# Channel-major products of a hybrid encoder layer as three 256-column matmuls into one sum, with the large operands at one byte offset

## The chip, the core and the metric

The kernel runs on one core of a Trainium2 chip. The engines of the core are TensorE (PE in the profile; PEld is its loading of weights), VectorE (DVE), ScalarE (ACT), GpSimd (POOL) and SyncE (SP). The metric is the device time of one launch in microseconds.

## What is computed

One layer of an encoder on 256 tokens of 2048 channels, all in float32. Cut to what matters here:

```python
n = rms_norm(h, norm_mix_w)
proj = einsum("bsd,dp->bsp", n, w_in)            # 2048 -> 13344 channels
#   q, k, v of 8 delta heads (conv, silu), z, gates; 3 branches of q, k, v for 8 dilated heads
mixed = concatenate([delta_mixer(...), dilated_mixer(...)], -1)
h = h + einsum("bsm,md->bsd", mixed, w_out)      # 2048 -> 2048
n = rms_norm(h, norm_ffn_w)
up = depthwise_conv_centered(einsum("bsd,df->bsf", n, w_ffn_in), conv_ffn_w)   # 2048 -> 11264
gate, val = split(up, 2, -1)
h = h + einsum("bsf,fd->bsd", silu(gate) * val, w_ffn_out)                     # 5632 -> 2048
return rms_norm(h, norm_final_w)
```

## The kernel before

Every float32 operand of the large products is split in two float32r numbers: a high part and the rest. A product is then three products: high x high, low x high and high x low. The activations n are kept transposed in `xcat`, a tile of 128 partitions x 16 slices k x 512 columns: of each slice the first 256 columns are the high part of the 256 tokens, the last 256 the low part.

Weights come from HBM in pieces of 1 MB into four buffers `raw`, issued from the SP queue (line 254). A piece serves two items (or two halves of a longer list). For each item ScalarE makes the high part (`hi`, line 263) and VectorE the rest (`lo`, line 264), 128 x 1024 elements each, in four buffers each, three items ahead of the matmuls (`LA = 3`). The order of the work on each engine is the order in which the program writes it. `run_items` walks over the items: it splits ahead, calls the `done` of the item before, issues the matmuls of this item, and then lets background generators (convolutions, the delta rule, attention, norms) issue some work, up to a budget per item on VectorE and ScalarE (`BV`, `BA`).

There are four kinds of large products:

- channel-major blocks (`cm_block`, lines 314 and 317): the weights are the stationary operand and `xcat` the moving one, so the result has channels on partitions. A block of 128 channels takes two items, with 16 steps over k. Each step is one matmul of 512 columns (`hi` against both halves of `xcat`) and one of 256 (`lo` against the first half). The 512 columns of the accumulator bank so hold two sums, which `evac` (lines 331 to 339) adds: ScalarE copies the second half into a small tile `tmp`, VectorE adds the first half and writes the result. 80 blocks of w_in and 88 blocks of w_ffn_in are made in this way, 2688 steps in all.
- token-major blocks of v (`v_slab`, lines 392 to 394): `xcat` is stationary, `hi` and `lo` are moving, 256 columns each, 1152 matmuls.
- w_out and w_ffn_out (`tm_group`, lines 1231 to 1233): `mxh`/`mxl` or `gth`/`gtl` are stationary, `hi` and `lo` moving, 512 columns each.
- a small product for the gates (lines 460 and 461), 32 channels wide, in 16 steps.

Blocks of w_in alternate between two accumulator banks, so the matmuls of a block wait until the block two before it has been read out. From the up-projection on there are four such banks. After the up-projection `up_hook` (lines 1380 to 1387) does as `evac` does, and then multiplies by `rbc` into a padded tile for the convolution.

The delta rule's solve, its scan and the attention run beside these products in the first half. The profile's lines L960 to L1050 are the scan, L1160 to L1211 the attention.

Of the kernel before, what the change touches and what calls it, by code (L numbers as in the profile page):

```python
# [4 lines left out]
F32 = mybir.dt.float32  # L5
F32R = mybir.dt.float32r
I32 = mybir.dt.int32
AF = mybir.ActivationFunctionType
ALU = mybir.AluOpType

P = 128
T = 256
D = 2048
KT = D // P
# [69 lines left out]
def block_kernel(tc, A, out, dbg=None):  # L84
# [4 lines left out]
    ACT = nc.scalar.activation  # L89
    V = nc.vector  # L90
    G = nc.gpsimd
    mm = nc.tensor.matmul
# [15 lines left out]
    def pool(name, **kw):  # L108
        g = tc.tile_pool(name=name, bufs=1, reuse_waits="tile", **kw)
        return g, g.__enter__()  # L110
# [5 lines left out]
    gw, wp = pool("weights", side="left")  # L116
    gx, xp = pool("xcat", side="right")
# [25 lines left out]
    raws = [wp.tile([P, 2048], F32, name=f"raw{i}") for i in range(NR)]  # L143
    his = [wp.tile([P, 1024], F32R, name=f"hi{i}") for i in range(NU)]
    los = [wp.tile([P, 1024], F32R, name=f"lo{i}") for i in range(NU)]
    tmps = [wp.tile([P, T], F32, name=f"tmp{i}") for i in range(2)]
    xcat = xp.tile([P, KT, 512], F32R, name="xcat")

    rec_d = dram.tile([H, P, 1536], F32, name="rec_d")
    z_d = dram.tile([H, P, T], F32, name="z_d")  # L150
# [4 lines left out]


    gens = []
    state = {"tmp": 0, "n": 0, "v": 0.0, "a": 0.0}
    done = set()

    def spawn(g, prio=1):
        gens.append((prio, len(gens) + state["n"], g))
        state["n"] += 1000
        gens.sort(key=lambda t: t[:2])
# [40 lines left out]
    def grab(slots):  # L205
        n = 0
        while not slots.free:
            pump(1e9, 1e9)
            n += 1
            assert n < 10000  # L210
        if n:
            state["forced"] = state.get("forced", 0) + 1
        return slots.get()
# [83 lines left out]
    def next_acc():  # L297
        accn[0] += 1
        return accs[accn[0] % len(accs)]

    def cm_block(ch, j, done, width=P):

        box = {}

        def half(kh):
            def mms(hi, lo):
                if kh == 0:
                    box["acc"] = next_acc()
                acc = box["acc"][:width]
                for kk in range(8):  # L310
                    k = kh * 8 + kk

                    def a():
                        mm(acc[:, :512], lhsT=hi[:, kk, :], rhs=xcat[:, k, :], start=k == 0, stop=k == KT - 1)  # L314

                    def b():
                        mm(acc[:, :T], lhsT=lo[:, kk, :], rhs=xcat[:, k, :T], start=False, stop=False)  # L317

                    if k == KT - 1:
                        b(), a()  # L320
                    else:
                        a(), b()

            return mms

        for kh in range(2):
            Item(ch[kh], lambda t, j=j: t[:, :, j * width : (j + 1) * width], half(kh),
                 (lambda: done(box["acc"])) if kh else None)

    def evac(out_ap, acc, n=P, perm=None):  # L330

        tmp = tmps[state["tmp"] % 2]
        state["tmp"] += 1
        ACT(tmp[:n], acc[:n, T:512], AF.Copy)
        a, b = acc[:n, :T], tmp[:n]
        if perm:
            a = a.rearrange("p (c m) -> p c m", c=4)
            b = b.rearrange("p (c m) -> p c m", c=4)
        V.tensor_add(out_ap, a, b)  # L339

    def natural(ap):

# [21 lines left out]
    g_hi = x0.tile([P, KT, 32], F32R, name="g_hi")  # L364
# [91 lines left out]
    gacc = next_acc()  # L456

    def gate_mms(k2):
        for k in (2 * k2, 2 * k2 + 1):
            mm(gacc[:32, :512], lhsT=g_hi[:, k, :], rhs=xcat[:, k, :], start=k == 0, stop=False)  # L460
            mm(gacc[:32, :T], lhsT=g_lo[:, k, :], rhs=xcat[:, k, :T], start=False, stop=k == KT - 1)

    for k2 in range(8):
        bk = DB.get()
        for e in range(2):
            k = 2 * k2 + e
            for q in range(2):
                nc.tensor.transpose(bk[:, e * T + q * P : e * T + (q + 1) * P], xs[q][:, k * P : (k + 1) * P], ident)
        if k2 >= 3:
            gate_mms(k2 - 3)  # L470
        for e in range(2):
            k = 2 * k2 + e
            src = bk[:, e * T : (e + 1) * T]
            ACT(xcat[:, k, :T], src, AF.Copy, scale=nw_mix[:, k : k + 1])
        for e in range(2):
            k = 2 * k2 + e
            src = bk[:, e * T : (e + 1) * T]
            stt(xcat[:, k, T:], src, nw_mix[:, k : k + 1], xcat[:, k, :T].bitcast(F32), op0=ALU.mult, op1=ALU.subtract)
        DB.put(bk)
        if k2 in (4, 7):  # L480
            split(prog["split"])
            prog["split"] += 1
    run_items(1)
    for k2 in range(5, 8):
        gate_mms(k2)
# [15 lines left out]
    def gate_hook(acc):  # L501
        gg_, gpool = pool("gates", side="right")
        graw = gpool.tile([32, T], F32, name="graw")
        evac(natural(graw), acc, n=32, perm=True)
        spawn(g_gates(graw, gg_, gpool), 0)
# [155 lines left out]
    def qkv_hook(which, h, acc):  # L661
        pad = grab(pads)
        evac(natural(pad[:, 2 : T + 2]), acc, perm=True)
        spawn(g_conv(which, h, pad))
# [125 lines left out]
    def z_hook(h, acc):  # L790
        if h == 6:
            z_pads()
        pad = grab(pads)
        evac(natural(pad[:, 2 : T + 2]), acc, perm=True)

        def g():
            yield 0
            zt = yield from take(zts)
            ACT(zt[:, 64:T], pad[:, 2 : T - 62], AF.Silu)
            ACT(zt[:, 0:64], pad[:, T - 62 : T + 2], AF.Silu)  # L800
            pads.put(pad)
            nc.gpsimd.dma_start(z_d[h], zt)
            done.add(("z", h))
            later(4, lambda: zts.put(zt))
            yield (0, 450)

        spawn(g(), 0)
# [257 lines left out]
    gl, lp = pool("dil", side="right")  # L1065
# [3 lines left out]
    sms = [lp.tile([P, 512], F32, name=f"sm{i}") for i in range(2)]  # L1069
    PT = lp.tile([P, 4, 2, P], F32, name="PT")  # L1070
    smal = lp.tile([P, 2, 4], F32, name="smal")
    swap = [(i + 16) % 32 for i in range(32)]

    def g_tables():
# [185 lines left out]
    rbc = rC  # L1260
# [90 lines left out]
    for c in range(2):  # L1351
        k0 = FT - 8 + 4 * c
        ch = Chunk(w_down[k0 * P : (k0 + 4) * P, 3 * 512 :].rearrange("(k p) c -> p k c", p=P), (4, 512))
        for u in range(2):
            i = 2 * c + u
# [23 lines left out]

    def up_hook(which, f, acc):  # L1380
        pad = grab(fpad)
        tmp = tmps[state["tmp"] % 2]
        state["tmp"] += 1
        ACT(tmp, acc[:, T:512], AF.Copy)
        V.tensor_add(tmp, acc[:, :T], tmp)
        V.tensor_mul(pad[:, 1 : T + 1], tmp, rbc)
        spawn(g_up(which, f, pad))

    hooks["up"] = up_hook
# [2 lines left out]
    def g_up(which, f, pad):  # L1392
        yield 0
        y = yield from take(fy)
        b = which * FT + f
        ACT(y, pad[:, 0:T], AF.Copy, scale=cwf[:, 0, b : b + 1])
        yield 0
        for d in (1, 2):
            stt(y, pad[:, d : d + T], cwf[:, d, b : b + 1], y, op0=ALU.mult, op1=ALU.add)  # L1399
        fpad.put(pad)  # L1400
        yield 700
        if which == 0:
            ACT(y, y, AF.Silu)
            gate_t[f] = y
            yield 0
        else:
            while f not in gate_t:
                yield 0
            g = gate_t.pop(f)
            V.tensor_mul(y, y, g)  # L1410
            fy.put(g)
            yield 300
            ACT(gth[:, f, :], y, AF.Copy)
            V.tensor_sub(gtl[:, f, :], y, gth[:, f, :].bitcast(F32))
            fy.put(y)
            yield 700
# [79 lines left out]
```

## Time and profile before

| | us |
|---|---|
| median of 3 runs | 1555.35 (1553.68 to 1556.74) |
| the profiled execution | 1554.66 |
| its span | 1552.9 |
| PE busy | 1522.1 (98%) |
| PEld busy | 1326.1 (85%) |
| DVE busy | 1102.1 (71%) |
| ACT busy | 848.3 (55%) |
| matmuls of lines 314 and 317 | 2688 each |
| matmuls of lines 392 to 394 | 384 each |
| matmuls of lines 1231 to 1233 with mxh, mxl | 128 each |

Matmuls overlap in the profile: a record is longer than the time after which the next one starts (a 128x512 matmul lasts 398 ns on average). What a matmul takes of the path is read from the distance between two starts, or from how many start in a window, and not from the duration of one.

### The profile page before, as it was taken

The page shows a single profiled execution, that of the slowest core. Times are in us where ns is not written, and L with a number is a line of the kernel's source. Part 1 is how long each engine was busy: PE and PEld are TensorE (multiplying, and loading weights), DVE is VectorE, ACT ScalarE, POOL GpSimd, SP SyncE. Part 2 cuts the span into 40 slices and gives each one's busy share as a digit, 9 for nine tenths or more (in the row PEclk, how much of TensorE's full clock was granted, in tenths as well). Part 3 has the DMA queues.
Part 4 walks back from the last instruction along what each step waited for, and adds up shares of the span by engine and source line. Part 5 has one row for each costly group of instructions (what it writes and reads, how often), then busy time and mean ns, then how long its engine had stood idle before and what let it go on. Part 6 is the DMA issues. An engine that isn't in the chain of part 4 may idle for free.

```text
span 1552.9 us, 23123 instructions
## 1 busy us (share of the span) xinstructions
PE 1522.1 (98%) x8827; PEld 1326.1 (85%) x8827; DVE 1102.1 (71%) x1872; ACT 848.3 (55%) x1518; POOL 163.4 (11%) x245
## 2 busy tenths in 40 slices
PE   7999997999999999999999999999999999999997
PEld 6878886898998898898788888888888888888886
DVE  5878986978965776676557777777777777455454
ACT  5587773555555555654546555555555555344342
POOL 3263442000012202100000000000000000000000
PEclk9999999999999999999999999999999999999999
DMA  9656689655658646554765555656565657566552
GB/s 256 217 171 207 221 264 216 215 172 163 190 145 243 217 129 197 183 163 160 245 205 177 191 189 184 196 170 210 165 206 173 202 179 246 198 211 211 191 190 81
DMA packets 247265, 300.88 MB, mean 194 GB/s; under 512 B 10981, under 2 KB 207766, under 8 KB 246770
## 3 DMA queue, kind: packets, MB, share of 16 engines
q1 hardware_dynamic: 235602, 269.81, 54.5%
q0 software_dynamic: 11120, 29.01, 6.2%
q8 instruction: 69, 1.13, 0.3%
q10 hardware_dynamic: 432, 0.59, 0.1%
q14 instruction: 42, 0.34, 0.1%
HBM read 285.69 MB, written 13.65 MB: 193 GB/s over the span
## 4 chain that ended last, share of the span: by engine, by line
PE 93%; DMA 2%; issue 1%; DVE 1%; ACT 1%; POOL 0%; POOLq 0%; SPq 0%; ACTq 0%; DVEq 0%
PE bank L314 38%; PE bank L317 19%; PE bank L1231 7%; PE bank L1232 7%; PE bank L1233 7%; PE bank L392 3%; PE bank L394 3%; PE bank L393 3%; DMA raw<-in_w_in_dram 2%; PE bank L989 1%; PE bank L1035 1%; PE bank L1030 1%; ACT kb L759 1%; DVE lo L264 0%; PE bank L1205 0%
## 5 line engine op out<-in xcount | busy, mean ns | idle before, releaser
L314 PE MATMUL bank<-xcat,hi 128*128 128x512 f32 x2688 | 950.7, 398 | 11.2 <-DVE qk L339 7.9
L264 DVE TENSOR_TENSOR lo<-raw,hi 128x1024 fp32r<-128x1024 f32 x504 | 620.1, 1232 | 351.9 <-ACT hi L263 348.0
L263 ACT ACTIVATE hi<-raw 128x1024 fp32r<-128x1024 f32 x504 | 533.2, 1059 | 535.9 <-PE bank L314 213.7
L317 PE MATMUL bank<-xcat,lo 128*128 128x256 f32 x2688 | 729.6, 282 | 0.0
L314 PEld LDWEIGHTS bank<-xcat,hi 128*128 128x128 f32 x2688 | 498.3, 189 | 118.7 <-DVE qk L339 8.2
L317 PEld LDWEIGHTS bank<-xcat,lo 128*128 128x128 f32 x2688 | 506.2, 188 | 13.5
L1231 PE MATMUL bank<-hi,gth 128*128 128x512 f32 x336 | 130.7, 389 | 0.0
L1233 PE MATMUL bank<-hi,gtl 128*128 128x512 f32 x336 | 130.7, 389 | 0.0
L1232 PE MATMUL bank<-lo,gth 128*128 128x512 f32 x336 | 130.7, 389 | 0.0
L392 PE MATMUL bank<-hi,xcat 128*128 128x256 f32 x384 | 108.6, 283 | 0.0
L394 PE MATMUL bank<-hi,xcat 128*128 128x256 f32 x384 | 106.5, 277 | 0.0
L393 PE MATMUL bank<-lo,xcat 128*128 128x256 f32 x384 | 106.4, 277 | 0.0
L1399 DVE SCALAR_TENSOR_TENSOR fy<-fpad,cwf,fy 128x256 f32<-128x256 f32 x176 | 84.8, 482 | 3.1
L1231 PEld LDWEIGHTS bank<-hi,gth 128*128 128x128 f32 x336 | 63.1, 188 | 13.1
L1233 PEld LDWEIGHTS bank<-hi,gtl 128*128 128x128 f32 x336 | 63.1, 188 | 13.1
L1232 PEld LDWEIGHTS bank<-lo,gth 128*128 128x128 f32 x336 | 63.1, 188 | 13.0
L392 PEld LDWEIGHTS bank<-hi,xcat 128*128 128x128 f32 x384 | 72.2, 188 | 0.5
L394 PEld LDWEIGHTS bank<-hi,xcat 128*128 128x128 f32 x384 | 72.4, 189 | 0.0
L393 PEld LDWEIGHTS bank<-lo,xcat 128*128 128x128 f32 x384 | 72.2, 188 | 0.1
L1231 PE MATMUL bank<-hi,mxh 128*128 128x512 f32 x128 | 51.4, 401 | 0.3 <-DVE hs L1269 0.3
L1429 POOL DMA_DIRECT2D nfb<-in_norm_final_w_dram x1 | 0.6, 590 | 483.3 <-PE bank L314 483.3
L1233 PE MATMUL bank<-hi,mxl 128*128 128x512 f32 x128 | 50.6, 395 | 0.0
(293 smaller groups left out, 1414.3 us busy)
## 6 DMA issues: line engine op xcount, KB each, us to landing
raw<-in_w_in_dram SPq DMA_DIRECT2D x104, 1024.0 KB, 5.5
raw<-in_w_ffn_in_dram SPq DMA_DIRECT2D x88, 1024.0 KB, 5.2
raw<-in_w_ffn_out_dram SPq DMA_DIRECT2D x44, 1024.0 KB, 5.0
raw<-in_w_out_dram SPq DMA_DIRECT2D x14, 1024.0 KB, 5.5
rec_d<-rec POOLq DMA_DIRECT2D x8, 768.0 KB, 6.7
rr<-rec_d POOLq DMA_DIRECT2D x6, 512.0 KB, 5.3
xt<-in_x_dram SPq DMA_DIRECT2D x4, 512.0 KB, 7.8
gam<-cg_d POOLq DMA_DIRECT2D x8, 256.0 KB, 8.2
```

Source lines behind the costliest of these rows:

```text
L263: ACT(hi, src, AF.Copy)
L264: V.tensor_sub(lo, src, hi.bitcast(F32))
L314: mm(acc[:, :512], lhsT=hi[:, kk, :], rhs=xcat[:, k, :], start=k == 0, stop=k == KT - 1)
L317: mm(acc[:, :T], lhsT=lo[:, kk, :], rhs=xcat[:, k, :T], start=False, stop=False)
L392: mm(o, lhsT=xh, rhs=hi[:, kk, :], start=k == 0 and t == 0, stop=False, skip_group_check=True)
L393: mm(o, lhsT=xh, rhs=lo[:, kk, :], start=False, stop=False, skip_group_check=True)
L394: mm(o, lhsT=xl, rhs=hi[:, kk, :], start=False, stop=k == KT - 1, skip_group_check=True)
L759: ACT(kb[sl, q, :], bk[sl, X * P + hf * 64 : X * P + hf * 64 + 64], AF.Copy, scale=bre[sl, 1, h, q : q + 1])
L1231: mm(a[t], lhsT=xh, rhs=hi[:, kk, :], start=st, stop=False)
L1232: mm(a[t], lhsT=xh, rhs=lo[:, kk, :], start=False, stop=False)
L1233: mm(a[t], lhsT=xl, rhs=hi[:, kk, :], start=False, stop=sp_)
L1399: stt(y, pad[:, d : d + T], cwf[:, d, b : b + 1], y, op0=ALU.mult, op1=ALU.add)
```

## The change

In `cm_block` the matmul of 512 columns becomes two of 256 with the same weights, and all three matmuls of a step add into the same 256 columns of the accumulator. The gates' product is written in the same way. `evac` then needs no second sum: ScalarE alone copies the 256 columns to their place, with the permutation where there is one, and VectorE's addition is gone. In `up_hook` ScalarE's copy and VectorE's addition are both gone, and the multiplication by `rbc` reads the accumulator itself. The two tiles `tmp` are gone.

Two unused tiles, `xgap` (320 bytes per partition) and `lgap` (480), move others. In the built program `raw`, `hi`, `lo`, `gth` and `gtl` start at 160 modulo 512 bytes in each partition, before and after. `xcat` starts at 480 before and at 160 after, `mxh` and `mxl` at 448 before and at 160 after, and so do the tiles of the attention (`qk`, `vv`, `sm`, `PT`).

```diff
+    xp.tile([P, 80], F32, name="xgap")
...
-                acc = box["acc"][:width]
+                acc = box["acc"][:width, :T]
                 for kk in range(8):
                     k = kh * 8 + kk
...
-                        mm(acc[:, :512], lhsT=hi[:, kk, :], rhs=xcat[:, k, :], start=k == 0, stop=k == KT - 1)
...
-                        mm(acc[:, :T], lhsT=lo[:, kk, :], rhs=xcat[:, k, :T], start=False, stop=False)
...
+                    mm(acc, lhsT=hi[:, kk, :], rhs=xcat[:, k, :T], start=k == 0, stop=False)
+                    mm(acc, lhsT=hi[:, kk, :], rhs=xcat[:, k, T:], start=False, stop=False)
+                    mm(acc, lhsT=lo[:, kk, :], rhs=xcat[:, k, :T], start=False, stop=k == KT - 1)
...
     def evac(out_ap, acc, n=P, perm=None):
-        tmp = tmps[state["tmp"] % 2]
-        state["tmp"] += 1
-        ACT(tmp[:n], acc[:n, T:512], AF.Copy)
-        a, b = acc[:n, :T], tmp[:n]
+        a = acc[:n, :T]
         if perm:
             a = a.rearrange("p (c m) -> p c m", c=4)
-            b = b.rearrange("p (c m) -> p c m", c=4)
-        V.tensor_add(out_ap, a, b)
+        ACT(out_ap, a, AF.Copy)
...
+    lp.tile([P, 120], F32, name="lgap")
...
     def up_hook(which, f, acc):
         pad = grab(fpad)
-        tmp = tmps[state["tmp"] % 2]
-        state["tmp"] += 1
-        ACT(tmp, acc[:, T:512], AF.Copy)
-        V.tensor_add(tmp, acc[:, :T], tmp)
-        V.tensor_mul(pad[:, 1 : T + 1], tmp, rbc)
+        V.tensor_mul(pad[:, 1 : T + 1], acc[:, :T], rbc)
```

What stands in a row on TensorE at the start of a block of the first stage (`bank_72` is the block's accumulator, `hi_100` and `lo_104` are the split weights of its first item), before:

```order
L314 MATMUL bank_72<-xcat,hi_100 128x512
L317 MATMUL bank_72<-xcat,lo_104 128x256
L314 MATMUL bank_72<-xcat,hi_100 128x512
L317 MATMUL bank_72<-xcat,lo_104 128x256
L314 MATMUL bank_72<-xcat,hi_100 128x512
```

and after:

```order
L313 MATMUL bank_72<-xcat,hi_100 128x256
L314 MATMUL bank_72<-xcat,hi_100 128x256
L315 MATMUL bank_72<-xcat,lo_104 128x256
L313 MATMUL bank_72<-xcat,hi_100 128x256
L314 MATMUL bank_72<-xcat,hi_100 128x256
```

A step over k is three instructions of 256 columns in place of one of 512 and one of 256; nothing else moves on this engine.

On VectorE in the first stage, where a block is read out between the splits of the weights (`rec` and `gam` belong to the delta rule), before:

```order
L765 TENSOR_TENSOR rec_359<-bank_73,gam_375 64x2x64 x4
L264 TENSOR_TENSOR lo_104<-raw_96,hi_100 128x1024
L264 TENSOR_TENSOR lo_105<-raw_97,hi_101 128x1024
L339 TENSOR_TENSOR pad_334<-bank_72,tmp_106 128x4x64
L264 TENSOR_TENSOR lo_102<-raw_94,hi_98 128x1024
```

and after:

```order
L755 TENSOR_TENSOR rec_382<-bank_73,gam_398 64x2x64 x4
L265 TENSOR_TENSOR lo_104<-raw_96,hi_100 128x1024
L265 TENSOR_TENSOR lo_105<-raw_97,hi_101 128x1024
L265 TENSOR_TENSOR lo_102<-raw_94,hi_98 128x1024
L265 TENSOR_TENSOR lo_103<-raw_95,hi_99 128x1024
```

The addition that freed the accumulator stood behind two splits on this engine, and is gone from it.

The same place on ScalarE, before:

```order
L263 ACTIVATE hi_100<-raw_96 128x1024
L602 ACTIVATE gam_377<-gam_377,ex 128x128 x4
L263 ACTIVATE hi_101<-raw_97 128x1024
L334 ACTIVATE tmp_106<-bank_72 128x256
L602 ACTIVATE gam_378<-gam_378,ex 128x128 x4
```

and after:

```order
L264 ACTIVATE hi_100<-raw_96 128x1024
L592 ACTIVATE gam_400<-gam_400,ex 128x128 x4
L264 ACTIVATE hi_101<-raw_97 128x1024
L328 ACTIVATE pad_357<-bank_72 128x4x64
L592 ACTIVATE gam_401<-gam_401,ex 128x128 x4
```

The copy stands where it stood, and now writes the padded tile itself. On all engines the rest of the order is the same as before, the issues of the SP and POOL queues included.

## Rows read from the trace of the kernel before

**Rows 1.** Page, part 1: busy us (share of the span) xinstructions of each engine

```profile
PE 1522.1 (98%) x8827; PEld 1326.1 (85%) x8827; DVE 1102.1 (71%) x1872; ACT 848.3 (55%) x1518; POOL 163.4 (11%) x245
```

**Rows 2.** Page, part 4: the chain that ended last, by engine

```profile
PE 93%; DMA 2%; issue 1%; DVE 1%; ACT 1%; POOL 0%; POOLq 0%; SPq 0%; ACTq 0%; DVEq 0%
```

**Rows 3.** Waits of PE for others: us in total, times, longest

```profile
PE bank L314 <- DVE qk L339: 7.9, 1, 7.9
...
PE bank L314 <- DVE pad L339: 2.3, 1, 2.3
...
PE bank L314 <- DVE xpad L339: 1.0, 1, 1.0
```

**Rows 4.** Windows: length, busy us (xinstructions) by engine, PE clock, DMA share, GB/s

```profile
860.00:1300.00 440.00, 440.00 (x2506) 383.90 (x2505) 340.85 (x549) 244.61 (x391) 0.00 (x0) 1.00 0.58 188
1310.00:1510.00 200.00, 200.00 (x884) 165.66 (x883) 100.15 (x93) 83.69 (x88) 1.42 (x2) 1.00 0.62 205
80.00:120.00 40.00, 37.67 (x214) 31.82 (x213) 29.42 (x51) 34.78 (x85) 23.31 (x26) 0.96 0.54 171
```

**Rows 5.** Timeline of PE in a channel-major block: start us, us, instruction

```profile
400.04 0.39 PE L314 MATMUL bank<-xcat,hi 128*128 128x512 f32 x1
400.27 0.28 PE L317 MATMUL bank<-xcat,lo 128*128 128x256 f32 x1
...
401.44 0.39 PE L314 MATMUL bank<-xcat,hi 128*128 128x512 f32 x1
```

**Rows 6.** Timeline of PE in a block of v, 17 matmuls from first to last

```profile
304.78 0.28 PE L393 MATMUL bank<-lo,xcat 128*128 128x256 f32 x1
304.90 0.28 PE L394 MATMUL bank<-hi,xcat 128*128 128x256 f32 x1
...
306.60 0.28 PE L394 MATMUL bank<-hi,xcat 128*128 128x256 f32 x1
```

**Rows 7.** Timeline of PE in the w_out product, 7 matmuls from first to last

```profile
739.66 0.40 PE L1232 MATMUL bank<-lo,mxh 128*128 128x512 f32 x1
...
741.06 0.40 PE L1232 MATMUL bank<-lo,mxh 128*128 128x512 f32 x1
```

**Rows 8.** Timeline of PE in the w_ffn_out product, 7 matmuls from first to last

```profile
1399.77 0.39 PE L1231 MATMUL bank<-hi,gth 128*128 128x512 f32 x1
...
1401.13 0.39 PE L1231 MATMUL bank<-hi,gth 128*128 128x512 f32 x1
```

**Rows 9.** Groups of ACT instructions: busy us, mean ns of one, idle before

```profile
L334 ACT ACTIVATE tmp<-bank 128x256 f32<-128x256 f32 x80 | 29.6, 370 | 0.1
...
L1210 ACT ACTIVATE mxh<-bank 128x256 fp32r<-128x256 f32 x8 | 5.0, 629 | 24.8 <-PE bank L1205 24.8
```

**Rows 10.** Groups of DVE instructions, the same columns

```profile
L1385 DVE TENSOR_TENSOR tmp<-bank,tmp 128x256 f32<-128x256 f32 x88 | 36.7, 417 | 0.0
...
L339 DVE TENSOR_TENSOR pad<-bank,tmp 128x256 f32<-128x256 f32 x19 | 11.7, 617 | 0.2
```

**Rows 11.** Timeline of PE around its first long stall

```profile
95.23 0.80 PE L314 MATMUL bank<-xcat,hi 128*128 128x512 f32 x1 [2.27 <-DVE pad L339]
...
96.04 0.63 PE L314 MATMUL bank<-xcat,hi 128*128 128x512 f32 x1
...
96.68 0.63 PE L314 MATMUL bank<-xcat,hi 128*128 128x512 f32 x1
```

**Rows 12.** Timeline of ACT at the same stall

```profile
92.17 0.38 ACT L334 ACTIVATE tmp<-bank 128x256 f32<-128x256 f32 x1
```

**Rows 13.** Timeline of DVE at the same stall

```profile
94.56 0.62 DVE L339 TENSOR_TENSOR pad<-bank,tmp 128x256 f32<-128x256 f32 x1
```

**Rows 14.** Timeline of ACT at the longest stall of PE

```profile
266.62 1.06 ACT L263 ACTIVATE hi<-raw 128x1024 fp32r<-128x1024 f32 x1 [10.92 <-DMA raw<-in_w_in_dram]
267.58 0.37 ACT L334 ACTIVATE tmp<-bank 128x256 f32<-128x256 f32 x1
```

**Rows 15.** Timeline of DVE at the longest stall of PE

```profile
268.85 0.42 DVE L339 TENSOR_TENSOR qk<-bank,tmp 128x256 f32<-128x256 f32 x1
```

More of the change, by code (lines that the diff above doesn't have):

```diff
@@ L145, in block_kernel @@
     los = [wp.tile([P, 1024], F32R, name=f"lo{i}") for i in range(NU)]
-    tmps = [wp.tile([P, T], F32, name=f"tmp{i}") for i in range(2)]
     xcat = xp.tile([P, KT, 512], F32R, name="xcat")
+    xp.tile([P, 80], F32, name="xgap")
     rec_d = dram.tile([H, P, 1536], F32, name="rec_d")
@@ L157, in block_kernel @@
     gens = []
-    state = {"tmp": 0, "n": 0, "v": 0.0, "a": 0.0}
+    state = {"n": 0, "v": 0.0, "a": 0.0}
     done = set()
@@ L308, in mms @@
                     box["acc"] = next_acc()
-                acc = box["acc"][:width]
+                acc = box["acc"][:width, :T]
                 for kk in range(8):
                     k = kh * 8 + kk
-                    def a():
-                        mm(acc[:, :512], lhsT=hi[:, kk, :], rhs=xcat[:, k, :], start=k == 0, stop=k == KT - 1)
-                    def b():
-                        mm(acc[:, :T], lhsT=lo[:, kk, :], rhs=xcat[:, k, :T], start=False, stop=False)
[L319 to L322, printed above, removed]
+                    mm(acc, lhsT=hi[:, kk, :], rhs=xcat[:, k, :T], start=k == 0, stop=False)
+                    mm(acc, lhsT=hi[:, kk, :], rhs=xcat[:, k, T:], start=False, stop=False)
+                    mm(acc, lhsT=lo[:, kk, :], rhs=xcat[:, k, :T], start=False, stop=k == KT - 1)
             return mms
@@ L459, in gate_mms @@
         for k in (2 * k2, 2 * k2 + 1):
-            mm(gacc[:32, :512], lhsT=g_hi[:, k, :], rhs=xcat[:, k, :], start=k == 0, stop=False)
+            mm(gacc[:32, :T], lhsT=g_hi[:, k, :], rhs=xcat[:, k, :T], start=k == 0, stop=False)
+            mm(gacc[:32, :T], lhsT=g_hi[:, k, :], rhs=xcat[:, k, T:], start=False, stop=False)
             mm(gacc[:32, :T], lhsT=g_lo[:, k, :], rhs=xcat[:, k, :T], start=False, stop=k == KT - 1)
```

## The prediction

> **What bounds the kernel now.** I read the shares of the engines first, then the chain of waits, then what PE waits for, and last the starts of single matmuls. PE is busy for 98% of the span [rows 1], and 93% of the chain that ended last is PE's own work [rows 2]. What it waits for on other engines behind a channel-major block comes to 7.9 + 2.3 + 1.0 = 11.2 us, and each of these three waits is for the addition of line 339 [rows 3]. So this is a kernel of matmuls in a row, and the price of the change is the distance from one matmul's start to the next, times how many there are. As many weight loads as matmuls are counted, 8827 [rows 1]: a matmul that keeps its weights loads them again all the same, so the second `hi` matmul of a step will too.
>
> Four distances can be read. In a channel-major step, from `hi` to `lo` 0.23 us and from one `hi` to the next (401.44 - 400.04) / 4 = 350 ns, which leaves 0.12 us for the `lo` matmul of 256 columns [rows 5]. Over 440 us of the up-projection 2506 / 2 = 1253 steps start [rows 4], so 351.2 ns each; this is the value that I use. In the blocks of v, where all matmuls have 256 columns: (306.60 - 304.78) / 16 = 113.75 ns [rows 6]. In w_out, 512 columns: (741.06 - 739.66) / 6 = 233.3 ns [rows 7]. In w_ffn_out, also 512 columns: (1401.13 - 1399.77) / 6 = 226.7 ns [rows 8], and over 200 us 884 matmuls start [rows 4], 226.2 ns each.
>
> The last two differ in one thing that the change touches. They are the same loop and the same moving tiles `hi` and `lo`, which start at 160 modulo 512 bytes; the stationary tile starts at 448 in w_out and at 160 in w_ffn_out. Where both start alike a 512-column matmul takes 226.7 ns, where not 233.3. The 512-column matmul of the channel-major step, with moving tile at 480 and weights at 160, takes 0.23 us [rows 5] and belongs with either by its rounding; the 351.2 of the step says that its two matmuls together lie above one and a half times 226.7, which is 340.
>
> **The change part by part.**
>
> *The steps.* 512 + 256 columns become 3 x 256; the columns stay 768. What three of 256 cost with all tiles at 160 no row shows. The nearest rows are the blocks of v, also three matmuls of 256 columns into one accumulator with new weights each time: 3 x 113.75 = 341.3 ns, with tiles not yet alike [rows 6]. Half of the 512-column matmul with tiles alike gives 3 x 113.3 = 340 ns [rows 8]. The end on the other side is the present `lo` matmul: 3 x 0.12 us = 360 ns, or, if the 512-column matmul is taken at w_out's 233.3, 3 x (351.2 - 233.3) = 354 ns [rows 4, 5, 7]. I take 340.5, between the two first, since both show the same thing in two ways: a fixed cost per matmul that is near nothing (113.75 is half of 226.7 to within a nanosecond). That is 10.7 ns per step, x 2688 = 28.8 us less. The ends: 30 us less at 340, 24 us more at 360. All of it lies on the path, since in the 440 us of the up-projection PE has no idle time [rows 4].
>
> *The other tiles.* w_out's 384 matmuls go from 233.3 to 226.7 if the offset is the cause: 6.6 x 384 = 2.5 us less (ends: 0 and 2.5). The 1152 matmuls of v go from 113.75 to 113.5 at most, 0.3 us. The gates' 16 steps: 16 x 11 ns, 0.2 us.
>
> *Reading out a block.* VectorE loses an addition of 417 ns, or 617 ns where it permutes [rows 10], in 168 blocks. This is work beside PE's, and worth nothing by itself; it counts where PE waits for the accumulator. ScalarE's copy stays for w_in's 80 blocks at 370 ns, and where it now permutes I take the 629 ns of the nearest copy that writes such an order [rows 9]. That is 0.26 us more in 32 blocks, hidden behind 5.4 us of matmuls per block as long as ScalarE has room. It is tightest between 80 and 120 us, busy 34.78 of 40 us [rows 4]; seven blocks there add 1.8 us, and the stretch shrinks by about 1.2, so it comes to some 94%. If that cover were gone, the steps' gain of these 40 us, about 1.2 us, would not show.
>
> *The three stalls.* At 92 us ScalarE's copy ends at 92.55 [rows 12], VectorE's addition only at 95.18 [rows 13], and PE starts at 95.23 [rows 11]. After the change the copy is the last thing, at about 92.17 + 0.63 = 92.8. But PE by then runs ahead by some 190 steps x 10.7 ns = 2 us, and ScalarE, full in this stretch, does not. So here stall and steps together give about 2.4 us, of which 2.0 are already in the sum: 0.4 remain, and the slow steps after the stall, 96.68 - 96.04 = 0.64 us in place of 0.35, the lower of the two clock levels (1.2 GHz, 0.96 of full over the stretch) [rows 4, 11], some 4 of them, 1.2 us, may stay or go. I take half, 0.6. The stall of 1.0 us [rows 3] I take as gone. At 267 us the weights land late, and this stays; but the bank is free after ScalarE's copy at 267.95 [rows 14] and not after the addition at 269.27 [rows 15], 1.3 us earlier, less some 0.6 that PE gains on the DMA before it: 0.7. Together 2.7 us (ends: 0 and 6).
>
> *What is hidden.* In the up-projection VectorE is busy 341 of 440 us and ScalarE 245 [rows 4]; both lose work there, and the stretch becomes 3% shorter, so neither becomes late. The queues of SP and POOL keep their order.
>
> *The sum.* 28.8 + 2.5 + 0.5 + 2.7 = 34.5 us. The profiled execution took 1554.66 us, the median is 1555.35; from the first 1520, from the second 1521. The first way of reading the offset (340 ns) would give 1519, and I give 1519 since the v rows too should lose what lies between them and it.
>
> **The rivals.**
>
> *The offset does nothing for 256 columns, and each matmul has a fixed cost.* Then w_out's 233.3 against 226.7 has some other cause, and the step is three times the present `lo` matmul: 354 to 360 ns, in the middle 357, 5.8 x 2688 = 15.6 us more, less 2.7 of the stalls: about 1568 us. The point from which this decides is a distance of 117 ns per matmul (351.2 / 3). For it: the one 256-column matmul with `xcat` moving takes 0.12 us [rows 5]. Against it: the v rows at 113.75, whose tiles do not start alike either [rows 6]. Chance 0.08. The Trainium skill, "TensorE: Matmul & The Clock Gate", section "Back-to-back issue gap", has a rule of this kind: a gap of N / 2.4 + 2.5 ns at full clock, so a fixed 2.5 ns for each matmul. By it the step would be 325 ns now and 327.5 after, 6.7 us more in all; the trace does not agree with its size, since it has 113.75 ns for 256 columns and 226.7 for 512, in proportion to the columns.
>
> *Half of it.* The offset removes only a part, and a matmul of 256 takes 115 to 116 ns: 345 to 348 ns, 9 to 17 us less in steps, with 5 us of the rest about 1537 us. For it: within the v rows the first two starts are 0.12 us apart where the mean is 113.75 ns [rows 6], so something may disturb single ones. Chance 0.12.
>
> *ScalarE becomes the bound of the first stage.* It has the copies to itself, and between 80 and 200 us it is the fullest engine beside PE. Then the steps' gain of that stage, some 120 us x 3% = 3.6 us, and the stalls' 2.7 go: about 1525 us. Chance 0.05, and inside the range.
>
> *The change does not do what it says.* The offsets are those of the built program, and the order of the instructions is as wanted, so this can only be the first rival.
>
> **How the numbers follow.** The forecast of 1519 has a chance of 0.75, the half 0.12, ScalarE 0.05, the slower case 0.08. The range reaches from 1509 (336 ns per step, 10 us below, since nothing shows that 113.3 is the least that a 256-column matmul with tiles alike can take, and the stalls' upper end) to 1541, the upper end of the half. About 0.2% is what a measurement of this kernel can tell from no change, 3 us. Faster by more: 0.91; slower by more: 0.08; between: 0.01.
>
> **What would show it.** In the changed kernel 860 to 1290 us should hold three matmuls per 340.5 ns, some 8.8 per us, with starts 0.11 apart, and the distances should hardly vary. w_out should have starts 0.227 apart. The waits of PE for line 339 should be gone, with one of some 7 us for ScalarE's copy near 260 us in their place. The prediction is wrong in its main term if the three matmuls of a step start 0.117 us apart or more, and in its smaller ones if PE waits for ScalarE between 80 and 240 us.

## The result, and the profile after

The change made the kernel slower: 1570.05 us against 1554.76 us for the kernel before in the same comparison, a ratio of 1.0102 with the interval [1.0086, 1.0118]. The spans of the two profiled executions are 1567.9 and 1552.9 us, 15.0 us apart.

Parts 1, 4 and 5 of the page of the changed kernel: busy time by engine, the chain by engine, and the three matmuls of a step. They answer to [rows 1, 2].

```profile
PE 1546.8 (99%) x11531; PEld 1477.6 (94%) x11531; DVE 1041.9 (66%) x1703; ACT 827.5 (53%) x1430; POOL 164.8 (11%) x245
...
PE 94%; DMA 3%; issue 1%; ACT 1%; POOL 1%; DVE 1%; POOLq 0%; SPq 0%; ACTq 0%; DVEq 0%
...
L313 PE MATMUL bank<-xcat,hi 128*128 128x256 f32 x2688 | 767.6, 286 | 2.9 <-ACT qk L328 2.9
L315 PE MATMUL bank<-xcat,lo 128*128 128x256 f32 x2688 | 761.1, 283 | 0.0
L314 PE MATMUL bank<-xcat,hi 128*128 128x256 f32 x2688 | 761.1, 283 | 0.0
```

VectorE lost 60 us of work, ScalarE 21, and PE's own work is 94% of the chain. So the answer lies in the distances of the matmuls. Timeline of PE in a channel-major block after (start us, us, instruction; 13 matmuls from first to last), against [rows 5]:

```profile
400.04 0.28 PE L313 MATMUL bank<-xcat,hi 128*128 128x256 f32 x1
400.16 0.28 PE L314 MATMUL bank<-xcat,hi 128*128 128x256 f32 x1
...
401.48 0.28 PE L313 MATMUL bank<-xcat,hi 128*128 128x256 f32 x1
```

(401.48 - 400.04) / 12 = 120 ns each, not 113.5. A block of v after, 9 matmuls, against [rows 6], and w_out, 8 matmuls, against [rows 7]:

```profile
303.83 0.28 PE L381 MATMUL bank<-hi,xcat 128*128 128x256 f32 x1
303.95 0.28 PE L382 MATMUL bank<-lo,xcat 128*128 128x256 f32 x1
...
304.79 0.28 PE L383 MATMUL bank<-hi,xcat 128*128 128x256 f32 x1
```

```profile
739.74 0.39 PE L1223 MATMUL bank<-lo,mxh 128*128 128x512 f32 x1
...
741.32 0.39 PE L1224 MATMUL bank<-hi,mxl 128*128 128x512 f32 x1
```

v went from 113.75 to (304.79 - 303.83) / 8 = 120 ns, although its code is untouched. w_out went from 233.3 to (741.32 - 739.74) / 7 = 225.7 ns. The same shift of tiles came with faster 512-column matmuls and slower 256-column matmuls.

Three windows after and one of the kernel before, the last (length, then busy us and instructions of PE, PEld, DVE, ACT, POOL, then PE clock, DMA share, GB/s), and PE's only wait behind a channel-major block, against [rows 3, 4]:

```profile
80.00:120.00 40.00, 40.00 (x339) 39.37 (x339) 29.26 (x50) 38.00 (x96) 23.80 (x26) 1.00 0.60 189
...
240.00:280.00 40.00, 37.11 (x297) 36.91 (x296) 27.45 (x51) 18.64 (x29) 5.61 (x9) 0.96 0.99 209
...
860.00:1290.00 430.00, 430.00 (x3586) 430.00 (x3585) 298.80 (x449) 211.10 (x300) 0.00 (x0) 1.00 0.56 185
...
240.00:280.00 40.00, 32.14 (x175) 27.74 (x174) 26.59 (x53) 16.48 (x28) 7.43 (x12) 0.91 0.98 211
```

```profile
PE bank L313 <- ACT qk L328: 2.9, 1, 2.9
```

Three matmuls take 430 / 3586 x 3 = 359.7 ns in the up-projection, where the step took 351.2. The stalls shrank by more than was forecast: 11.2 us of waits became 2.9, the stretch from 80 to 120 us has no idle PE and no time at the lower clock level (1.00 in place of 0.96), and ScalarE fills 38.00 of its 40 us without becoming late.

### The profile page after: what moved, and what is told of

Same layout as the page of the kernel before. It is cut to its first block, busy times and chain, and to the rows that moved or that the text cites. A ratio compares the mean times of both kernels' runs of the same rounds, so it can differ in the third digit from the quotient of the medians.

```text
span 1567.9 us, 28173 instructions
## 1 busy us (share of the span) xinstructions
PE 1546.8 (99%) x11531; PEld 1477.6 (94%) x11531; DVE 1041.9 (66%) x1703; ACT 827.5 (53%) x1430; POOL 164.8 (11%) x245
## 4 chain that ended last, share of the span: by engine, by line
PE 94%; DMA 3%; issue 1%; ACT 1%; POOL 1%; DVE 1%; POOLq 0%; SPq 0%; ACTq 0%; DVEq 0%
PE bank L313 19%; PE bank L314 19%; PE bank L315 19%; PE bank L1222 7%; PE bank L1224 7%; PE bank L1223 7%; PE bank L381 3%; PE bank L383 3%; PE bank L382 3%; DMA raw<-in_w_in_dram 1%; PE bank L979 1%; PE bank L1025 1%; PE bank L1020 1%; DMA Bt<-a_d 1%; DMA xt<-in_x_dram 0%
## 5 line engine op out<-in xcount | busy, mean ns | idle before, releaser
L313 PE MATMUL bank<-xcat,hi 128*128 128x256 f32 x2688 | 767.6, 286 | 2.9 <-ACT qk L328 2.9
L315 PE MATMUL bank<-xcat,lo 128*128 128x256 f32 x2688 | 761.1, 283 | 0.0
L314 PE MATMUL bank<-xcat,hi 128*128 128x256 f32 x2688 | 761.1, 283 | 0.0
L313 PEld LDWEIGHTS bank<-xcat,hi 128*128 128x128 f32 x2688 | 516.1, 192 | 5.3 <-ACT qk L328 3.1
L314 PEld LDWEIGHTS bank<-xcat,hi 128*128 128x128 f32 x2688 | 516.4, 192 | 0.0
L315 PEld LDWEIGHTS bank<-xcat,lo 128*128 128x128 f32 x2688 | 516.1, 192 | 0.0
L381 PE MATMUL bank<-hi,xcat 128*128 128x256 f32 x384 | 110.6, 288 | 0.0
L383 PE MATMUL bank<-hi,xcat 128*128 128x256 f32 x384 | 108.6, 283 | 0.0
```

The costliest lines, as they stand in the source:

```text
L313: mm(acc, lhsT=hi[:, kk, :], rhs=xcat[:, k, :T], start=k == 0, stop=False)
L314: mm(acc, lhsT=hi[:, kk, :], rhs=xcat[:, k, T:], start=False, stop=False)
L315: mm(acc, lhsT=lo[:, kk, :], rhs=xcat[:, k, :T], start=False, stop=k == KT - 1)
L381: mm(o, lhsT=xh, rhs=hi[:, kk, :], start=k == 0 and t == 0, stop=False, skip_group_check=True)
L383: mm(o, lhsT=xl, rhs=hi[:, kk, :], start=False, stop=k == KT - 1, skip_group_check=True)
```

## The experiments

**The two halves of the change apart.** `gap_only` is the kernel before with the two unused tiles alone; `split_only` is the changed kernel without them.

```diff
 gap_only, against the kernel before
+    xp.tile([P, 80], F32, name="xgap")
...
+    lp.tile([P, 120], F32, name="lgap")
```

```diff
 split_only, against the changed kernel
-    xp.tile([P, 80], F32, name="xgap")
...
-    lp.tile([P, 120], F32, name="lgap")
```

> The kernel before with the two unused tiles alone: 512 and 256 columns per step as before, xcat and mxh now at 160 modulo 512 like hi and lo. Theory A (a matmul costs its columns at 2.4 GHz plus a fixed time that the relation of the two start offsets sets, 13.3 ns where they are alike): a step takes 226.7 + 120 = 347 ns, the 256-column matmuls of v go from 113.75 up to 120, w_out goes from 233.3 down to 226.7. Sum: -4.5 ns x 2688 = -12, +6.2 ns x 1152 = +7, -2.5: about 1547 us. Rival B (the offset does nothing to 256 columns, v became slower from something else in the changed kernel): v stays at 113.75, a step takes 226.7 + 118 = 345 ns, about 1536 us.

> The changed kernel without the two unused tiles: three matmuls of 256 columns and the shorter read-out, xcat at 480 and mxh at 448 as before. Theory A: v goes back to 113.75, w_out to 233.3, and a step takes three times what the one 256-column matmul took before, 3 x 118 to 119 = 354 to 357 ns: +3 to +6 ns x 2688 = +8 to +15, less 4 for the stalls: 1559 to 1567 us. Rival B: v stays at 120 (it is the company of more matmuls that slows it), a step 360 ns, 1572 us or more.

`gap_only`: 1561.42 us, ratio 1.0038 [1.0023, 1.0053]. `split_only`: 1549.79 us, ratio 0.9961 [0.9948, 0.9973]. The up-projection of both (columns as above):

```profile
860.00:1290.00 430.00, 430.00 (x2436) 372.93 (x2435) 331.56 (x533) 238.09 (x382) 0.00 (x0) 1.00 0.58 186
```

```profile
860.00:1290.00 430.00, 430.00 (x3653) 430.00 (x3652) 304.07 (x457) 215.14 (x306) 0.00 (x0) 1.00 0.57 187
```

So each half alone: the offsets make the old step 430 / 1218 = 353.0 ns, slower by 1.8; the cut alone makes it 3 x 117.7 = 353.1 ns. Both together make 359.7. v is at 119.8 ns in `gap_only` and at 114.4 in `split_only` (means of the starts next to each other in the trace), so its slowing is the offset's, and rival B is out. Theory A missed in `gap_only`, where it wanted 347 ns: in the up-projection the 512-column matmul, in turn with one of 256, is at 236 there and not at 227, the 256-column one at 117 and not at 120. Theory A missed in `split_only` too, which it wanted slower than before, at 1559 to 1567 us. The offsets were the harmful half. The other half is faster although its steps are not (353.1 ns against 351.2); what it gains is looked for in its read-out below.

**The offsets by themselves.** `sweep` holds nothing but matmuls: sixteen moving tiles, each 32 bytes further modulo 512 from the weights than the one before, three patterns with each.

> A kernel that computes nothing of the reference: weights at 160 modulo 512, and sixteen moving tiles xa to xp that start 0, 32, 64, ... 480 bytes further modulo 512; with each 96 matmuls of 256 columns in the order of the changed step, 64 of 512 columns, and 32 steps of 512 + 256. Theory A: the distance of two starts depends on the tile; 256 columns take 120 ns with xa, 113 to 114 with xg (the relation that v had before), 118 to 119 with xk (that of the channel-major step before); 512 columns 227 with xa and 233 with xh (that of w_out before). Rival B: the tile does not matter, 256 columns take the same with all sixteen.

For some tiles, the matmuls of 256 columns in threes (L51 is the first of three; 32 of them), those of 512 (L55), and of one tile those of 512 in turn with 256 (L58); the row gives first and last start in us:

```profile
L55 PE MATMUL bank<-xa,hi x64: 389/389/398, 44.4 to 58.7; 128*128 128x512 f32 x64
L51 PE MATMUL bank<-xa,hi x32: 280/283/283, 32.9 to 44.0; 128*128 128x256 f32 x32
L58 PE MATMUL bank<-xa,hi x32: 389/398/403, 58.9 to 69.8; 128*128 128x512 f32 x32
...
L51 PE MATMUL bank<-xc,hi x32: 278/279/279, 107.5 to 118.5; 128*128 128x256 f32 x32
...
L51 PE MATMUL bank<-xd,hi x32: 279/279/286, 144.8 to 155.9; 128*128 128x256 f32 x32
...
L55 PE MATMUL bank<-xg,hi x64: 388/396/398, 268.2 to 282.9; 128*128 128x512 f32 x64
L51 PE MATMUL bank<-xg,hi x32: 276/276/283, 257.3 to 267.9; 128*128 128x256 f32 x32
...
L51 PE MATMUL bank<-xi,hi x32: 280/283/283, 332.0 to 343.2; 128*128 128x256 f32 x32
...
L51 PE MATMUL bank<-xk,hi x32: 278/279/279, 406.7 to 417.6; 128*128 128x256 f32 x32
...
L51 PE MATMUL bank<-xo,hi x32: 276/276/283, 556.5 to 567.0; 128*128 128x256 f32 x32
```

With 93 distances between the first starts of the first and the last three: relation 0 (xa) 11.1 / 93 = 119 ns, 64 (xc) 118, 96 (xd) 119 again, 192 (xg) 10.6 / 93 = 114; and the same again 256 bytes further (xi 120, xk 117, xo 113). For 512 columns 0 and 192 change places: relation 0 14.3 / 63 = 227 ns, relation 192 14.7 / 63 = 233. Theory A held: the relation modulo 256 decides, the cheapest one for 256 columns is among the dearest for 512, and a moving tile that starts like the weights is, with the one 96 bytes further, the worst for 256. The durations in the rows tell 0 and 192 apart too: 276 ns for a record at 113, 283 at 120. The third pattern, 512 and 256 columns in turn, takes (69.8 - 58.9) / 31 = 352 ns at relation 0, so the 353.0 of `gap_only` is that of the matmuls alone: in turn with another width a matmul does not keep the distance that it has among its own kind. The sweep moves only the moving tile. That it is the relation of both, v shows: its moving tiles stayed at 160, only the stationary `xcat` moved, and v went to 120.

**The best relation in the kernel.** `split192` shifts the tiles so that `xcat` is 192 past `hi` and `lo`; `split192v` also writes the splits for v 128 bytes further; `gap192` is the old form of the step at those offsets.

```diff
 split192, against the changed kernel
-    xp.tile([P, 80], F32, name="xgap")
+    xp.tile([P, 32], F32, name="xgap")
...
-    lp.tile([P, 120], F32, name="lgap")
+    lp.tile([P, 40], F32, name="lgap")
```

```diff
 split192v, on top of that
-    his = [wp.tile([P, 1024], F32R, name=f"hi{i}") for i in range(NU)]
+    his = [wp.tile([P, 1088], F32R, name=f"hi{i}") for i in range(NU)]
...
-        hi = his[u % NU][:, : a * b].rearrange("p (a b) -> p a b", a=a)
+        hi = his[u % NU][:, it.off : it.off + a * b].rearrange("p (a b) -> p a b", a=a)
...
-                 (lambda: done(box["acc"])) if u == 3 else None)
+                 (lambda: done(box["acc"])) if u == 3 else None, 32)
```

> The changed kernel with xcat at 352 modulo 512, so 192 bytes past hi and lo modulo 256, and mxh at 160 as in the changed kernel. The sweep gave 113 to 114 ns for 256 columns at that relation. Theory A' (the fixed time follows the relation modulo 256, the same in the kernel as in the sweep): a step 3 x 113.5 = 340.5 ns against 360, so -19 x 2688 = -52 us against the changed kernel; v, where the relation is then 64, 117.7 instead of 120, -2.5 us: 1515 us. Rival C (the step is held at 118 or more by something else once xcat moves, as traffic into the same memory): at most what split_only gives, 1548 us.

> As split192, and the splits of v's weights are written 128 bytes further in buffers that are 256 bytes longer, so v too has the relation 192. Theory A': v goes from 117.7 to 113.5, 1152 x 4.2 = 4.8 us less than split192: about 1510 us. Rival C: no difference.

> The kernel before, 512 and 256 columns per step, with the offsets of split192. The sweep gave 353 ns for such a step at this relation. Theory A': the relation that makes three matmuls fast does nothing for this form; steps +2 ns x 2688 = +5, v 117.7: +4, w_out -2.5: about 1562 us. If the offset alone were the gain, it would come out near 1520.

`split192`: 1544.24 us, 0.9939 [0.9923, 0.9956]. `split192v`: 1541.27 us, 0.9915 [0.9900, 0.9930]. `gap192`: 1558.78 us, 1.0031 [1.0018, 1.0044]. So the offset alone is no gain, it pays only together with the cut, and v gains 3 us more. But 1515 was expected of `split192`, and 1510 of `split192v`. In `split192v` the up-projection stood at 420 / 3569 = 117.7 ns per matmul:

```profile
860.00:1280.00 420.00, 420.00 (x3569) 420.00 (x3568) 297.19 (x446) 209.84 (x297) 0.00 (x0) 1.00 0.57 186
```

Item by item the trace showed two values only, 113.3 and 117.8 ns, in stretches: in `split192` 113.3 from 277 to 294 us and from 350 to 399, and 117.8 from 812 to 1290 without a break. It changed where matmuls of another kind (transposes, the scan, attention, the border to a block of v) or a stall came between.

**What in a matmul the relation acts on.**

> A kernel that computes nothing of the reference. Weights hi at 160, moving tiles xa (relation 0) and xg (relation 192), a second weight tile un to which xa has the relation 192. With xa and xg: 96 matmuls each of 128, 256, 384 and 512 columns, then 256 columns with weights of 32 columns; then 256 columns with hi and un in turn; then with xa and xg in turn. Theory D (what disturbs a matmul is the loading of the next matmul's weights while it streams): with hi and un in turn on xa, the matmul with un, behind which hi is loaded, takes 120, and that with hi 113.5; with weights of 32 columns the fixed time mostly goes. Rival E (it is its own weights' offset): hi 120, un 113.5, and 32 columns change nothing.

The rows of `partner`, 96 matmuls in each group (95 distances), L55 with 128 columns, L57 256, L59 384, L61 512, L63 256 with weights of 32 columns:

```profile
L55 PE MATMUL bank<-xa,hi x96: 221/274/277, 24.8 to 35.4; 128*128 128x128 f32 x96
L57 PE MATMUL bank<-xa,hi x96: 274/283/334, 35.5 to 46.9; 128*128 128x256 f32 x96
L59 PE MATMUL bank<-xa,hi x96: 334/334/339, 47.1 to 63.5; 128*128 128x384 f32 x96
L61 PE MATMUL bank<-xa,hi x96: 387/389/397, 63.7 to 85.3; 128*128 128x512 f32 x96
L63 PE MATMUL bank<-xa,hi x96: 280/280/281, 85.5 to 96.7; 128*32 128x256 f32 x96
```

```profile
L57 PE MATMUL bank<-xg,hi x96: 276/276/331, 130.1 to 140.9; 128*128 128x256 f32 x96
L59 PE MATMUL bank<-xg,hi x96: 332/335/335, 141.0 to 157.5; 128*128 128x384 f32 x96
L61 PE MATMUL bank<-xg,hi x96: 392/395/398, 157.7 to 179.8; 128*128 128x512 f32 x96
```

At relation 0: 120, 173 and 227 ns for 256, 384 and 512 columns, so 53.5 ns for each 128 columns and about 13 on top of every matmul from 256 columns up. At relation 192: 114, 174, 233: the part on top is 7, 13 and 19. With 128 columns it is 112 ns at relation 0, hardly less than 256 columns take at the good relation. Weights of 32 columns change little (118 in place of 120). With two weight tiles in turn on xa the matmul with hi took 117.5 ns and that with un 119.2, and with xa and xg in turn both took 117, so neither D nor E held: the time is not the next weights' nor its own weights' alone. Why the two starts matter stays open.

**The read-out.** `old_readout` cuts the matmul in two but keeps the two sums, the copies and the additions, at the old offsets.

```diff
 old_readout, against the kernel before
-                        mm(acc[:, :512], lhsT=hi[:, kk, :], rhs=xcat[:, k, :], start=k == 0, stop=k == KT - 1)
...
+                    mm(acc[:, :T], lhsT=hi[:, kk, :], rhs=xcat[:, k, :T], start=k == 0, stop=False, skip_group_check=True)
+                    mm(acc[:, T:], lhsT=hi[:, kk, :], rhs=xcat[:, k, T:], start=False, stop=False, skip_group_check=True)
...
```

> The kernel before, its offsets too, with the 512-column matmul cut in two of 256 that go into the two halves of the bank, so the two sums, ScalarE's copies and VectorE's additions all stay. Theory H (the read-out's shorter way out of the accumulator is worth some 9 us, which is why split_only was faster than before although its step is not): steps as in split_only, 353 ns, so +1.8 ns x 2688 = +5: about 1560 us, with PE's waits for line 339 back at some 11 us. Rival I (split_only's gain is the three matmuls' own): about 1550 us.

1558.54 us, 1.0025 [1.0015, 1.0036], as theory H wanted. Against `split_only` that is 0.64% or about 9.9 us. The matmuls have the same widths and offsets in both (3653 in 430 us of the up-projection); beside the read-out they differ only in the half of the bank that the second `hi` matmul adds to. The difference arises in the first stage: the first matmul of v starts at 306.9 us in `old_readout` and at 296.7 in `split_only`. PE's waits in `old_readout`, and then in `split_only` (us in total, times, longest):

```profile
PE bank L313 <- DVE qk L332: 7.4, 1, 7.4
...
PE bank L313 <- DVE pad L332: 2.2, 1, 2.2
...
PE bank L313 <- DVE xpad L332: 1.0, 1, 1.0
```

```profile
PE bank L312 <- ACT qk L327: 4.5, 1, 4.5
```

The waits make 10.6 - 4.5 = 6.1 us of it. A part of the rest is the clock: the granted clock is 0.96 over 80 to 120 us and 0.91 over 240 to 280 in `old_readout`, 1.00 and 0.96 in `split_only`; after a long wait PE ran for some us at the lower of its two levels (1.2 GHz, as in [rows 11]).

**The two cadences.** `kicks` adds to `split192v` a few matmuls of other widths, whose result nobody reads; `kicks_old` and `kicks_alike` add the same ones at the old offsets and at those of the changed kernel; `tuned` and `four` choose places and numbers.

```diff
 kicks, against split192v
+    kicks = {"n": 0, 180: (128,), 200: (128, 128), 220: (128, 128, 128), 240: (384,), 260: (64,),
+             280: (128,) * 4, 300: (128,) * 8, 320: (512,)}
...
+                for n in kicks.get(kicks["n"], ()):
+                    mm(banks[5][:, :n], lhsT=hi[:, 0, :], rhs=xcat[:, kh * 8, :n], start=True, stop=True)
```

> split192v with a few extra matmuls whose result nobody reads, each at the start of one item of the up-projection: at the 20th item one of 128 columns, at the 40th two, the 60th three, the 80th one of 384, the 100th one of 64, the 120th four of 128, the 140th eight of 128, the 160th one of 512. In split192 and split192v the step sat at one of two cadences, 3 x 113.3 or 3 x 117.8 ns, for stretches of up to 480 us, and changed only where another kind of matmul came between. Theory F (two stable cadences, picked by how the stream of matmuls happens to start after an interruption): at least some of these extra matmuls, 0.1 to 0.9 us each, switch the following 20 items from 117.8 to 113.3 or back. Rival G (the cadence of the up-projection is set by the traffic of its stage): it stays at 117.8 throughout.

`kicks` took 1531.95 us in one run. The first of its extra matmuls, with the matmuls around it, and windows of the up-projection:

```profile
848.25 0.28 PE L321 MATMUL bank<-xcat,hi 128*128 128x256 f32 x1
848.37 0.28 PE L322 MATMUL bank<-xcat,lo 128*128 128x256 f32 x1
848.49 0.22 PE L317 MATMUL bank<-xcat,hi 128*128 128x128 f32 x1
848.55 0.34 PE L320 MATMUL bank<-xcat,hi 128*128 128x256 f32 x1
```

```profile
860.00:960.00 100.00, 100.00 (x885) 100.00 (x884) 73.13 (x110) 51.61 (x73) 0.00 (x0) 1.00 0.58 190
1075.00:1120.00 45.00, 45.00 (x385) 45.00 (x384) 31.76 (x49) 22.61 (x32) 0.00 (x0) 1.00 0.57 185
1130.00:1230.00 100.00, 100.00 (x885) 100.00 (x884) 72.28 (x110) 52.03 (x74) 0.00 (x0) 1.00 0.60 193
1240.00:1280.00 40.00, 40.00 (x342) 40.00 (x341) 28.77 (x45) 20.22 (x29) 0.00 (x0) 1.00 0.56 190
```

One matmul of 128 columns at 848 us turned 117.8 into 113.3; the one of 64 at 1067 turned it back (45 / 385 = 117 ns), the four at 1124 made it 113 again, the one of 512 at 1234 ended it. The others (two and three of 128, one of 384, eight of 128) found 113.3 and left it so. The traffic of the stage is nearly the same in all four windows (185 to 193 GB/s). Theory F holds, and G is out.

> split_only, so xcat at 480 and the relation 320 (64 modulo 256), with the extra matmuls of the run kicks at the same items. If both cadences exist at this relation too (some distances of 113 stood among its 118), those of 128 columns bring the up-projection to 113.3 here as well, and the offset of xcat was not needed: below 1540 us. If the relation decides which cadences there are, it stays at 117.8 and the run at about 1552.

> The changed kernel, all tiles alike, relation 0, with the extra matmuls of the run kicks. At this relation all 256-column matmuls took 120 ns in the changed kernel and in the sweep. If there is a single cadence at relation 0, the extra matmuls change nothing but their own 2 us: about 1572 us. If there is a faster one to be picked, the up-projection drops.

`kicks_old` took 1551.14 us and stayed at 430 / 3653 = 117.7 ns, `kicks_alike` 1574.9 us and stayed at 430 / 3586 = 119.9: the rows of their up-projections have the same counts as those of `split_only` and of the changed kernel.

```profile
860.00:1290.00 430.00, 430.00 (x3653) 429.95 (x3652) 303.12 (x456) 213.13 (x301) 0.00 (x0) 1.00 0.57 186
```

```profile
860.00:1290.00 430.00, 430.00 (x3586) 429.96 (x3586) 298.06 (x448) 209.11 (x296) 0.00 (x0) 1.00 0.56 182
```

So the relation decides which cadences were seen in the up-projection, and only at 192 an interruption picked between 113.3 and 117.8. That is not shown for every stream: in the first stage `kicks_old`, at relation 64, has stretches at 113.3 too (12 matmuls from 128.07 to 129.43 us).

> split192v with one extra matmul of 128 columns at each of six items: four between 200 and 290 us and two at the start of the up-projection, behind the last transposes of the norm. In the run kicks every such matmul of 128 columns was followed by the cadence 3 x 113.3 until the next other matmul. Theory F: the whole up-projection at 113.3, 1408 steps x 13.5 ns = 19 us less than split192v, and 2 to 4 us in the first stage: about 1519 us. Rival (the cadence falls back by itself): between this and 1541.

`tuned` missed: 1541.77 us, 0.9919 [0.9901, 0.9937]. Of its two extra matmuls at the start of the up-projection the one at 811 us brought 113.3, and the one at 817 us undid it. A single one toggled the cadence in all seven cases, the six of `tuned` and the first of `kicks`.

> split192v with four extra matmuls of 128 columns in a row at three items: two in the first stage and one at the start of the up-projection, behind the last transposes. In the runs kicks and tuned two or more in a row were always followed by the cadence 3 x 113.3, and a single one by the other cadence than the one before it (113.3 to 117.8 at 245 and 817 us, 117.8 to 113.3 at 224, 811 and 848 us). If that holds the whole up-projection runs at 113.3: 1408 x 13.5 ns = 19 us less than split192v's 1541, so about 1521 us. If it was chance which cadence followed, or the cadence falls back by itself, 1541.

`four`: 1526.93 us, 0.9824 [0.9807, 0.9842], and its up-projection is at 410 / 3620 = 113.3 ns from end to end. This version is faster than both kernels:

```profile
860.00:1270.00 410.00, 410.00 (x3620) 410.00 (x3619) 299.57 (x454) 213.29 (x302) 0.00 (x0) 1.00 0.60 193
```

It is 6 us short of what was expected. From its first step to its last the up-projection takes 480.6 us against 498.2 in `split192v`, 17.6 of the 19 us. The first stage gained nothing: the up-projection starts 2.6 us later, with a wait of 0.9 us for the bank of the extra matmuls, and with stretches that stayed at 117.8.

## Why the prediction was wrong, by its own steps

| term | forecast, us | as the runs show it, us |
|---|---|---|
| the steps | -28.8 (340.5 ns) | (359.7 - 351.2) x 2688 = +22.9 |
| v, gates | -0.5 | (120 - 113.75) x 1152 = +7.2, v alone |
| w_out | -2.5 | (225.7 - 233.3) x 384 = -2.9 |
| the stalls | -2.7 | waits 2.9 - 11.2 = -8.3 |
| sum | -34.5 | +18.9, where the spans differ by +15.0 |

The 4 us between the last two lie for the most part before v, whose first matmul starts at 304.7 us before and at 299.1 after, 5.6 us earlier, where the 704 steps up to there (+6.0) and the waits (-8.3) make 2.3. A part of it is the lower clock level behind the waits at 92 and 261 us: 0.96 over 80 to 120 us and 0.91 over 240 to 280 before, 1.00 and 0.96 after. By an estimate from these rows that is (0.04 + 0.05) x 40 = 3.6 us, some of which fell into the waits themselves.

*What bounds the kernel* was right, and so was, for the steps alone, the point from which the sign turns, 117 ns per matmul. It came out at 119.9. (With the read-out's gain the kernel as a whole turns a little later: `split_only` is at 117.7 and still 0.4% faster than before.)

*The steps* failed, and in one place: the value for three 256-column matmuls with tiles alike. It was taken from two rows that seemed to say the same, 113.75 ns in v [rows 6] and half of 226.7 ns in w_ffn_out [rows 8], and from their agreement a fixed cost of nearly nothing was read. The agreement was chance. Both rows hold a fixed part, 7 ns at v's relation of 192 with 256 columns, and 13 ns at w_ffn_out's relation of 0 with 512. v's relation happens to be the best of the sweep for 256 columns. Cutting a matmul of relation 0 in two doubles its 13 ns. No large product in the trace of before had 256 columns at relation 0, and the end of the range for that unknown (354 to 360 ns, from the present `lo` matmul) did contain the measured 359.7. The mistake was to give that end a chance of 0.08 when the argument against it was v, whose tiles the change was about to move. Even 113.75 was not all that v showed. Other blocks of v in the trace of before ran at 117.7 ns, as this one did, 23 matmuls from first to last, (676.85 - 674.26) / 22:

```profile
674.26 0.28 PE L393 MATMUL bank<-lo,xcat 128*128 128x256 f32 x1
...
676.85 0.28 PE L394 MATMUL bank<-hi,xcat 128*128 128x256 f32 x1
```

So both cadences could be read before the change, and the rows taken were of the faster one. (The v rows also do not have new weights each time, as was said: of the three matmuls of a step the first two use the same slice of `xcat`. A load is counted for each all the same.)

*v* failed with it: 0.3 us was taken "at most", when the same shift that the argument counted on for w_out could move v as well, in either direction.

*w_out* was right in mechanism and size.

*The stalls* were too small: PE's waits fell by 8.3 us and the shorter read-out is worth about 9.9 (`old_readout` against `split_only`), where 2.7 with an upper end of 6 were taken. I counted the stall at 92 us as nearly used up by PE's lead. There was no lead, since the steps became slower, so its whole 2.3 us came in. That the release moves from the addition to the copy was right. For the stall of 7.9 us near 261 us the mechanism was wrong: I took the landing of the weights as fixed. ScalarE's split that waits for them starts at 266.62 us before [rows 14], and the same split after at 257.59:

```profile
257.59 1.06 ACT L264 ACTIVATE hi<-raw 128x1024 fp32r<-128x1024 f32 x1 [3.45 <-DMA raw<-in_w_in_dram]
...
273.15 1.06 ACT L264 ACTIVATE hi<-raw 128x1024 fp32r<-128x1024 f32 x1 [1.99 <-DMA raw<-in_w_in_dram]
274.11 0.36 ACT L328 ACTIVATE qk<-bank 128x256 f32<-128x256 f32 x1
```

PE comes to that block about 1 us earlier than before, not later, and does not wait there. Its 2.9 us fall two blocks later, behind a split that gets its weights at 273.15 us. Why the first of these pieces landed 9 us earlier was not traced.

*The rivals.* The first named the time, 1568, and the form: a fixed cost per matmul. That its time came so near is partly luck: its step of 357 ns was too short, it had no loss in v, and it took 2.7 us for the stalls. And it wanted the offset without effect on 256 columns, and the offset had one, upward: 119.9 in the changed kernel, 117.7 without the gaps. The rule of the Trainium skill that stood beside it ("TensorE: Matmul & The Clock Gate", section "Back-to-back issue gap") has this form as well; its fixed 2.5 ns is some 13 in `partner` at relation 0. ScalarE as the bound did not come about: it is busy for 95% between 80 and 120 us, where 94% was estimated, and PE does not wait for it there.

What the forecast wanted can be had, at relation 192 and not at 0: `four` runs the up-projection at 113.3 ns per matmul, the 340 of the forecast, and takes 1526.93 us.

## What to carry to other kernels

A distance between matmuls belongs to its width and to the offsets of its two tiles together; rows of another width or another offset do not give it, and two of them that agree prove nothing. Where operands are moved, list every product that reads them and ask of each which way it goes. A shorter way from the last matmul of a block to the release of its accumulator can be worth more than the waits for it: some 9.9 us here, of which 6.1 were waits, because the release stood behind other work in an engine's queue.

## What had not been expected of the hardware

- For these float32r matmuls the distance depends on the start of the moving tile against that of the weights, with a period of 256 bytes: 113 to 120 ns for 256 columns and 227 to 234 for 512, in steps of 32 bytes, with the best place at 192 for 256 columns and at 0 for 512.
- A matmul of 128 columns with new weights each time takes 112 ns, against 114 to 120 for 256 columns (`partner`).
- At relation 192 the stream of the up-projection keeps one of two cadences, 113.3 or 117.8 ns, for hundreds of us; one matmul of 128 columns switched it in all seven cases where it stood alone, and two or more in a row were followed by 113.3 in each of the five cases in the up-projection, of which two found 117.8. Why is open.
